# Weights of the S5 scan inside the first feed-forward: products one step later, factors loaded earlier, the steps over 48 weight tiles instead of 32

## The chip, the cores and the metric

The kernel runs on one core of one Trainium2 chip. The metric is device microseconds (us) of one launch; a shorter time is better. Five engines take part: TensorE (PE, matrix products; its weight loads are shown as PEld), VectorE (DVE), ScalarE (ACT), GpSimd (POOL) and SyncE (SP), whose queue issues nearly all transfers. Each engine works through its own list of instructions in a fixed order, and so does each queue of transfers.

## The reference

Two blocks of two layers each act on 256 latent and 256 context tokens of width 1024. The first block ends each layer with a SwiGLU feed-forward, and the second layer of the second block is an S5 state-space mixer. Cut to what matters here:

```python
def _swiglu(h, w_gate, w_up, w_down):
    return (jax.nn.silu(h @ w_gate) * (h @ w_up)) @ w_down

def s5_discretize(a_re, a_im, b_re, b_im, c_re, c_im, log_dt):
...
    a_bar = jnp.exp(dt * a)
    b_bar = ((a_bar - 1) / a)[..., None] * lax.complex(f(b_re), f(b_im))
    c_mat = lax.complex(f(c_re), f(c_im))
    return a_bar, b_bar, c_mat

def s5_scan(u, a_bar, b_bar, c_mat, x0):
...
        bu = jnp.einsum('btgh,gph->btgp', u_blk.astype(jnp.complex64), b_bar)
...
        _, xs = lax.associative_scan(_affine_compose, (a, bu), axis=1)
        y = jnp.einsum('btgp,ghp->btgh', xs, c_mat).real
```

There are two directions, 64 groups of 16 channels and 64 states a group, and the S5 parameters don't depend on the tokens. So the kernel turns the recurrence into blocks of 8 tokens and makes the matrices of these blocks (powers of a_bar times b_bar, c_mat times powers of a_bar, and the products of both) ahead of time, while the first block's first feed-forward runs.

## The kernel before

All products run in float32 split in two parts: `split` (L195, L196) makes `hi` on ScalarE and `lo` on VectorE out of each loaded weight tile, and `mm3` (L205 to L207) multiplies hi by hi, hi by lo and lo by hi. A weight tile is 128 columns of output and up to 8 slices of 128 inputs, so it costs 24 products of 512 tokens each (21 with 7 slices). `linear_steps` runs over the tiles of one weight matrix: it loads and splits a tile, multiplies, hands the sum to a consumer, and then calls `tick`, which runs one step of a generator that lies in the background. The first three tiles of each matrix are multiplied in two halves of 256 tokens.

The first feed-forward (`ffn`, called in `body` with the weights `f0_u`, `f0_d0` to `f0_d2`) has three blocks. Block 0 has 16 gate and up tiles and then 8 down tiles of 8 slices; blocks 1 and 2 have 14 gate and up tiles and 8 down tiles of 7 slices. A gate tile is evicted by ScalarE as `sg` (L1683), an up tile by VectorE (L1687), which ScalarE and VectorE turn into the two parts `hh` (L1694) and `hl` (L1695); the down tiles multiply `hh` and `hl`, and VectorE puts their sums into `y` (L1706, L1708). The feed-forward is called with `ticks=("w", ())`: a tick follows each gate and up tile, and none follows a down tile.

`"w"` is the generator `s5_weights`. It runs over 16 chunks of 4 groups, and in each over two directions `d`. A chunk begins with the load of its factors `bc` (L1443, SP queue, two buffers). One direction is: three VectorE operations that make `Wt` (L1456 twice, L1457); four transposes of `Wt` on TensorE into PSUM (L1460), a copy `wvo` on ScalarE (L1463) and its store `wv` on the SP queue (L1464); three GpSimd operations that make `Ec` (L1471 twice, L1472) and the two stores `wc` of it on the SP queue (L1476); four products of `Ec` with the factors on TensorE (L1479). After the second direction VectorE builds `band` (L1486 to L1489) from these products, and GpSimd issues four stores `tt` of it (L1491). There is one step to each direction, so 32 ticks carry all of it: 16 in block 0, 14 in block 1 and 2 in block 2. The tile names draw on few buffers: two of `Wt` (both are in use while the sum is made), three of `Ec`, two of `bc`, two of `band` and two PSUM banks each of the kinds `pa` (transposes) and `pb` (products).

The order on the engines is not the order of the source: a planner takes the source as a list by priority and puts an instruction on its engine as soon as, by its own estimates, its inputs and buffers are there. That is why the first steps of the generator stand some 60 us ahead of the feed-forward's first tile.

Of the kernel before, what the change touches and what calls it, by code (L numbers as in the profile page):

```python
# [9 lines left out]
F32 = mybir.dt.float32  # L10
# [3 lines left out]
ALU = mybir.AluOpType  # L14
# [3 lines left out]
P = 128  # L18
# [6 lines left out]
SEGS = ((1, 0, CTX), (0, CTX, T))  # L25
# [12 lines left out]
def vw(ap, off, dims):  # L38
    return bass.AP(ap.tensor, ap.offset + off, [ap.ap[0]] + [list(d) for d in dims])
# [89 lines left out]
class Kern:  # L129
# [125 lines left out]
    def load(self, Wd):  # L255
        raw = self.wp.tile(list(Wd.shape), F32, tag="raw", name=self.n("raw"), bufs=4)
        self.nc.sync.dma_start(raw, Wd)
        return raw
# [1043 lines left out]
    def s5_poles(self, pool, sc, par):  # L1302
# [8 lines left out]
        def tt(a, b, op, out=None):  # L1311
            o = t() if out is None else out
            v.tensor_tensor(o, a, b, op)
            return o
# [41 lines left out]

        E = pool.tile([P, 6, 128], F32, tag="E", name="s5E")
        lo, hi = slice(0, 64), slice(64, 128)
        tt(e, co, ALU.mult, E[:, 0])
        ni = tt(e, sn, ALU.mult, sn)  # L1360
# [15 lines left out]
        for i, r, src, sign in ((1, lo, ni, -1.0), (1, hi, ni, 1.0), (2, lo, ph[0], 1.0), (2, hi, ph[1], -1.0),  # L1376
                                (3, lo, ph[1], -1.0), (3, hi, ph[0], -1.0), (4, lo, ph[1], 1.0), (4, hi, ph[0], -1.0),
                                (5, lo, ph[0], 1.0), (5, hi, ph[1], 1.0)):
            nc.scalar.mul(E[r, i], src[r], sign)
        nc.sync.dma_start(sc["E"], E)  # L1380

    def s5_powers(self, pool, sc):
# [4 lines left out]
        def tile(tag, n):  # L1387
            return pool.tile([P, 512], F32, tag=tag, name=self.n("s5p"), bufs=4)[:, :n * 128].rearrange("p (n c) -> p n c", n=n)

        E1, E2, w = tile("Pm", 4), tile("Pm", 2), tile("Pm", 2)  # L1390
        nc.sync.dma_start(E1, sc["E"][:, 0:4])
        nc.sync.dma_start(E2, sc["E"][:, 4:6])

# [41 lines left out]
    def s5_weights(self, pool, sc):  # L1435

        nc, A = self.nc, self.A
        PG = pool.tile([P, 4, 9, 128], F32, tag="PG", name="PGr")
        nc.sync.dma_start(PG, sc["pg"])
        PW, F1, F2 = [PG[:, 0], PG[:, 1]], PG[:, 2], PG[:, 3]  # L1440
        for ch in range(16):
            w = pool.tile([P, 560], F32, tag="bc", name=self.n("bc"), bufs=2)
            nc.sync.dma_start(w, A["s5_w"][ch])  # L1443
            BA = w[:, :160].rearrange("p (d g h) -> p d g h", d=2, g=5)
            BB, CA, CB = (w[:, o:o + 128].rearrange("p (d g h) -> p d g h", d=2, g=4) for o in (160, 288, 416))
            Dd = w[:, 544:560]
            kp = self.psum("pb")
            for d in range(2):
                o = 64 * d + 4 * ch

                base, st = (7 * 128, -128) if d == 0 else (0, 128)
                pw = [vw(PW[i], base + o, [[1, 4], [st, 8], [0, 16]]) for i in range(2)]
                bs = [x[:, d, :4, None, :].to_broadcast([P, 4, 8, 16]) for x in (BA, BB)]
                Wt = [pool.tile([P, 4, 8, 16], F32, tag="Wt", name=self.n("Wt"), bufs=2) for _ in range(2)]
                for i in range(2):
                    nc.vector.tensor_tensor(Wt[i], pw[i], bs[i], ALU.mult)  # L1456
                nc.vector.tensor_tensor(Wt[0], Wt[0], Wt[1], ALU.add)  # L1457
                ps = self.psum("pa")
                for g in range(4):
                    nc.tensor.transpose(ps[:, g * P:(g + 1) * P], Wt[0][:, g].rearrange("p s h -> p (s h)"),  # L1460
                                        self.ident)
                wv = pool.tile([P, 4, 128], F32, tag="wvo", name=self.n("wvo"), bufs=2)
                nc.scalar.copy(wv.rearrange("p g n -> p (g n)"), ps)  # L1463
                nc.sync.dma_start(sc["wv"][ch, :, :, d], wv)  # L1464

                base, st = (0, 128) if d == 0 else (8 * 128, -128)
                ff = [vw(f, base + o, [[1, 4], [st, 9], [0, 16]]) for f in (F1, F2)]
                cs = [x[:, d, :, None, :].to_broadcast([P, 4, 9, 16]) for x in (CA, CB)]
                Ec = [pool.tile([P, 4, 9, 16], F32, tag="Ec", name=self.n("Ec"), bufs=3) for _ in range(2)]
                for i in range(2):  # L1470
                    nc.gpsimd.tensor_tensor(Ec[i], ff[i], cs[i], ALU.mult)  # L1471
                nc.gpsimd.tensor_tensor(Ec[0], Ec[0], Ec[1], ALU.add)  # L1472
                E = Ec[0].rearrange("p g d h -> p g (d h)")
                for r in range(2):
                    rs = slice(64 * r, 64 * r + 64)
                    nc.sync.dma_start(sc["wc"][ch // 2, r, d, :, 4 * (ch % 2):4 * (ch % 2) + 4],  # L1476
                                      E[rs, :, 16:144] if d == 0 else E[rs, :, 0:128])
                for g in range(4):
                    nc.tensor.matmul(kp[32 * g:32 * g + 32, d * P:(d + 1) * P],  # L1479
                                     BA[:, d, g:g + 2, :].rearrange("p g h -> p (g h)"),  # L1480
                                     E[:, g, 0:128] if d == 0 else E[:, g, 16:144], start=True, stop=True,
                                     skip_group_check=True)
                if d == 0:
                    yield
            band = pool.tile([P, 240], F32, tag="band", name=self.n("band"), bufs=2)
            nc.vector.tensor_copy(band[:, 0:128], kp[:, 128:256])  # L1486
            nc.vector.tensor_tensor(band[:, 112:128], band[:, 112:128], Dd, ALU.add)
            nc.vector.tensor_tensor(band[:, 112:128], band[:, 112:128], kp[:, 0:16], ALU.add)
            nc.vector.tensor_copy(band[:, 128:240], kp[:, 16:128])  # L1489
            for j in range(4):  # L1490
                nc.gpsimd.dma_start(sc["tt"][ch // 2, :, :, 4 * (ch % 2) + j].rearrange("s h c -> h s c"),  # L1491
                                    vw(band[32 * j:32 * j + 16], 112, [[-16, 8], [1, 128]]))
            yield

    def s5_shift(self, shift, pool):

# [219 lines left out]
def body(tc, A, out, dbg=None):  # L1716
    with ExitStack() as ctx:
        K = Kern(tc, A, ctx, dbg)
        nc = K.nc
        K.load_pack()  # L1720
        xd = K.dr.tile([P, KT, T], F32, tag="xd", name="xd")
        sc = scratch(K)
        g = K.gains1
# [30 lines left out]
        with tc.tile_pool(name="ffn0", bufs=1) as fp:  # L1754
            x = fp.tile([P, KT, T], F32, tag="x", name="x")
            nc.sync.dma_start(x[:, :, :CTX], A["ctx1"])
            nc.sync.dma_start(x[:, :, CTX:], A["x"])
            y = fp.tile([P, KT, T], F32, tag="y", name="y0")
            acc = K.squares(SEGS)

            def mixed(i, ps, a, b, y=y, acc=acc):
                nc.vector.tensor_copy(y[:, i, a:b], ps)
                K.add_squares(acc, y, i, SEGS, a, b)

            step = K.halves(x, y, acc, lambda: (K.vecP(m0[:, :, 2], g[:, 0, 1]), K.vecA(m0[:, :, 4], g[:, 0, 2], "b"),
                                                m0[:, :, 3]))
            K.linear_fm(A["ew_out"], M, 512, mixed, ends=True, half=lambda: next(step))
            X = next(step)
            y = fp.tile([P, KT, T], F32, tag="y", name="y1")
            part = s1.rearrange("p k c -> p (k c)")[:, :32].rearrange("p (v j) -> p v j", v=2)  # L1770
            K.bg["w"] = K.s5_weights(fp, sc)
            acc = K.squares(SEGS)
            step = K.halves(x, y, acc, lambda: (K.vecP(m0[:, :, 5], g[:, 0, 3]), K.vecA(m1[:, :, 1], g[:, 1, 0], "b"),
                                                m1[:, :, 0]))

            def half():
                K.finish("w")
                next(step)

            K.ffn(X, 512, A["f0_u"], [A[f"f0_d{i}"] for i in range(3)], "swiglu", y, fp, 9,  # L1780
                  lambda k, a, b: K.add_squares(acc, y, k, SEGS, a, b), half=half, ticks=("w", ()))
            X = next(step)
            nc.sync.dma_start(xd[:, :, CTX:], x[:, :, CTX:])
        with tc.tile_pool(name="mix1", bufs=1) as mix:
# [4 lines left out]
        with tc.tile_pool(name="in2", bufs=1) as xp:  # L1789
# [5 lines left out]
            with tc.tile_pool(name="ffn1", bufs=1) as fp:  # L1795
                y = fp.tile([P, KT, LAT], F32, tag="y", name="y0")
                acc = K.squares(LSEG)
# [10 lines left out]
                acc = K.residual_rms(xl, y, K.vecP(m1[:, :, 2], g[:, 1, 1]), LSEG, acc)  # L1808
                X = K.norm_mod(xl, K.vecA(m1[:, :, 4], g[:, 1, 2], "b"), m1[:, :, 3], LSEG, acc)
                grp[1](pool=fp, bufs=8)  # L1810
                y = fp.tile([P, KT, LAT], F32, tag="y", name="y1")
# [11 lines left out]
                acc = K.residual_rms(xl, y, K.vecP(m1[:, :, 5], g[:, 1, 3]), LSEG, acc3)  # L1823
# [292 lines left out]
```

## Time and profile before

| | us |
|---|---|
| median of 3 runs | 2606.03 (2606.03, 2606.04, 2597.53) |
| the profiled execution | 2601.28 |
| its span on the core | 2599.5 |
| TensorE busy | 2427.1 (93%) |
| VectorE busy | 1513.9 (58%) |
| ScalarE busy | 972.1 (37%) |
| GpSimd busy | 514.6 (20%) |

The feed-forward's tiles run from 434 us to 896 us of the span, and the ticks with S5 work from there to 782 us. The profile tells each instruction's start and duration, what its engine waited for ahead of it, and in slices the clock that TensorE was granted (1.00 is full speed). "Busy" counts the time from an instruction's start to its end, including what it waits inside.

### The profile page before, as it was taken

To read this page: it belongs to the slowest core of one execution; us is meant where nothing else is said; L and a number is where in the kernel's file an instruction comes from. 1 tells how busy PE (TensorE), PEld (TensorE's weight loads), DVE (VectorE), ACT (ScalarE), POOL (GpSimd) and SP (SyncE) were. 2 spreads that over 40 slices of the span, in tenths; PEclk is the share of its full clock that TensorE was granted. 3 is DMA by queue.
4 is the path that set the end of the run, shared out by engine and by line. 5 is a ranking of instruction groups with operands and counts; after the bars stand their busy time and mean duration, and the time that the engine had idled before them with its cause. 6 is when DMAs were issued, how large, how long until landed. Compare 5 with 4: busy or idle time off the path is not lost.

```text
span 2599.5 us, 40143 instructions
## 1 busy us (share of the span) xinstructions
PE 2427.1 (93%) x15813; PEld 1979.1 (76%) x15813; DVE 1513.9 (58%) x2897; ACT 972.1 (37%) x1591; POOL 514.6 (20%) x648
## 2 busy tenths in 40 slices
PE   6999989989889998889999999999999999959999
PEld 5875566768678688889699788556888888628999
DVE  5545436865843466674555552665588744485666
ACT  5523323312222253333444453443423224534443
POOL 2910013763710042330100100110100000260000
PEclk9999999989999999999999999999999999989999
DMA  8326673654543332113665522002365533876564
GB/s 284 116 92 223 242 273 100 166 158 122 153 127 100 104 113 98 59 48 105 255 225 181 194 89 82 17 17 74 111 191 178 170 107 96 185 259 220 154 181 152
DMA packets 162925, 378.05 MB, mean 145 GB/s; under 512 B 24144, under 2 KB 70096, under 8 KB 162608
## 3 DMA queue, kind: packets, MB, share of 16 engines
q1 hardware_dynamic: 159728, 368.27, 44.3%
q0 software_dynamic: 3008, 7.21, 1.4%
q8 instruction: 125, 2.05, 0.3%
q14 instruction: 64, 0.52, 0.1%
HBM read 344.75 MB, written 30.67 MB: 144 GB/s over the span
## 4 chain that ended last, share of the span: by engine, by line
PE 73%; DVE 10%; DMA 6%; POOL 5%; ACT 3%; issue 2%; SPq 1%; POOLq 0%; DVEq 0%; ACTq 0%
PE pl L205 17%; PE pl L206 16%; PE pl L207 16%; PE pm L329 3%; POOL Ec L1471 2%; DMA bc<-s_w 2%; DVE lo L196 2%; PE pl L984 2%; PE pa L77 2%; DMA mcol<-ada_t 1%; POOL Ec L1472 1%; PE pl L279 1%; PE pl L280 1%; PE pl L277 1%; DVE pm L395 1%
## 5 line engine op out<-in xcount | busy, mean ns | idle before, releaser
L195 ACT CAST hi<-raw 128x1024 fp32r<-128x1024 f32 (+4 forms) x393 | 400.2, 1020 | 841.9 <-PE pl L206 640.3
L196 DVE TENSOR_TENSOR lo<-raw,hi 128x1024 fp32r<-128x1024 f32 (+4 forms) x393 | 486.6, 1240 | 341.1 <-ACT hi L195 334.9
L206 PE MATMUL pl<-X,hi 128*128 128x256 f32 (+1 forms) x2032 | 654.2, 323 | 5.9 <-POOL X L490 5.7
L205 PE MATMUL pl<-X,hi 128*128 128x256 f32 (+1 forms) x2032 | 657.6, 326 | 1.6 <-ACT X L487 1.6
L207 PE MATMUL pl<-X,lo 128*128 128x256 f32 (+1 forms) x2032 | 652.1, 322 | 1.5 <-DVE lo L196 1.5
L205 PEld LDWEIGHTS pl<-X,hi 128*128 128x128 f32 x2032 | 395.3, 195 | 39.3 <-issue 9.1
L206 PEld LDWEIGHTS pl<-X,hi 128*128 128x128 f32 x2032 | 395.7, 195 | 37.8 <-POOL X L490 8.6
L207 PEld LDWEIGHTS pl<-X,lo 128*128 128x128 f32 x2032 | 396.2, 195 | 33.4 <-issue 4.9
L205 PE MATMUL pl<-hh,hi 128*128 128x256 f32 (+1 forms) x1071 | 330.0, 309 | 10.7 <-ACT hh L1694 10.6
L206 PE MATMUL pl<-hl,hi 128*128 128x256 f32 (+1 forms) x1071 | 328.4, 307 | 8.5 <-DVE hl L1695 8.3
L207 PE MATMUL pl<-hh,lo 128*128 128x256 f32 (+1 forms) x1071 | 326.8, 306 | 0.0
L205 PEld LDWEIGHTS pl<-hh,hi 128*128 128x128 f32 x1071 | 203.7, 191 | 32.2 <-ACT hh L1694 12.2
L206 PEld LDWEIGHTS pl<-hl,hi 128*128 128x128 f32 x1071 | 204.1, 191 | 20.7 <-DVE hl L1695 10.6
L207 PEld LDWEIGHTS pl<-hh,lo 128*128 128x128 f32 x1071 | 204.4, 191 | 10.4 <-DVE y L1708 0.4
L1471 POOL TENSOR_TENSOR Ec<-PGr,bc 128x576 f32<-128x576 f32 x64 | 102.0, 1609 | 181.4 <-DVE lo L196 84.3
L205 PE MATMUL pl<-M,hi 128*128 128x256 f32 (+1 forms) x416 | 125.9, 305 | 6.9 <-ACT hi L195 5.9
L329 PE MATMUL pm<-mraw,s_cc 128*32 128x512 f32 x576 | 116.0, 606 | 10.3 <-DMA mraw<-ada_w 9.8
L207 PE MATMUL pl<-M,lo 128*128 128x256 f32 (+1 forms) x416 | 123.1, 297 | 1.2 <-DVE lo L196 1.2
L206 PE MATMUL pl<-M,hi 128*128 128x256 f32 (+1 forms) x416 | 123.5, 298 | 0.2 <-DVE M L856 0.2
L1708 DVE TENSOR_TENSOR y<-y,pl 128x256 f32<-128x256 f32 (+1 forms) x86 | 45.2, 526 | 127.2 <-PE pl L207 126.9
L490 POOL TENSOR_TENSOR X<-nt,X 128x256 fp32r<-128x256 f32 x48 | 37.4, 781 | 379.7 <-ACT nt L489 379.7
L395 DVE SCALAR_TENSOR_TENSOR pm<-mcol,mrow 128x512 f32<-128x512 f32 x128 | 89.3, 698 | 36.1 <-DMA mcol<-ada_t 22.4
(515 smaller groups left out, 3757.7 us busy)
## 6 DMA issues: line engine op xcount, KB each, us to landing
mraw<-mod_w SPq DMA_DIRECT2D x96, 512.0 KB, 5.5
raw<-f_u SPq DMA_DIRECT2D x88, 512.0 KB, 3.8
mraw<-ada_w SPq DMA_DIRECT2D x64, 512.0 KB, 6.3
raw<-p_u SPq DMA_DIRECT2D x64, 512.0 KB, 3.6
raw<-p_d SPq DMA_DIRECT2D x64, 512.0 KB, 3.6
raw<-ow_fm SPq DMA_DIRECT2D x32, 512.0 KB, 3.3
mcol<-ada_t SPq DMA_DIRECT2D x64, 256.0 KB, 3.1
raw<-f_d SPq DMA_DIRECT2D x32, 448.0 KB, 3.3
```

Source lines behind the costliest of these rows:

```text
L77: K.nc.tensor.matmul(self.ps[32 * j:32 * j + 32, :N], K.ones[:rows, :32], self.sq[:rows, :N], start=k < 4, stop=k + 4 >= self.kt, skip_gro ...
L195: nc.scalar.copy(hi, raw)
L196: nc.vector.tensor_tensor(lo, raw, f32(hi), ALU.subtract)
L205: mm(out, w[0][:, kw, wsl], xh, start=first and a == 0, stop=False, skip_group_check=True)
L206: mm(out, w[0][:, kw, wsl], xl, start=False, stop=False, skip_group_check=True)
L207: mm(out, w[1][:, kw, wsl], xh, start=False, stop=last and a == nk - 1, skip_group_check=True)
L329: nc.tensor.matmul(ps[32 * j:32 * j + 32, :], s[:, k, :], raw[:, jj * 512:(jj + 1) * 512], start=k == 0, stop=k == KT - 1, skip_group_chec ...
L395: nc.vector.scalar_tensor_tensor(self.psum("pm"), buf[:, n % 2], 1.0, s[:, v], ALU.mult, ALU.mult, accum_out=(dst if h else part)[:, v, j: ...
L490: nc.gpsimd.tensor_tensor(lo[:, k, a:b], t, f32(hi[:, k, a:b]), ALU.subtract)
L984: nc.tensor.matmul(ps[:, :nk], q[:, tt * P:(tt + 1) * P], k[:, :nk], start=True, stop=True)
L1471: nc.gpsimd.tensor_tensor(Ec[i], ff[i], cs[i], ALU.mult)
L1708: nc.vector.tensor_tensor(y[:, c, a0:b0], y[:, c, a0:b0], ps, ALU.add)
```

## The change

`s5_weights` is cut in two. A new function `products` holds the transposes, the copy and store of `wvo`, the stores `wc`, the products of `Ec`, and after the second direction `band` and the stores `tt`. A step now first runs `products` for the step before it, and then makes `Wt` and `Ec` of its own; the last products follow the loop. The load of `bc` is taken out of the chunk's head: the first stands ahead of the loop, and each next chunk's is issued in the second direction's step of the chunk before it, behind the products of that step. After a second direction there are two yields instead of one, so that a chunk takes three ticks (two with work, one empty), and the feed-forward is called with ticks after down tiles too: 48 ticks and a last one, over 16 + 8 + 14 + 8 tiles and the first three of block 2.

```diff
-        for ch in range(16):
+        def load(ch):
             w = pool.tile([P, 560], F32, tag="bc", name=self.n("bc"), bufs=2)
             nc.sync.dma_start(w, A["s5_w"][ch])
...
+            return w
+
+        def products(ch, Wt, E, BA, Dd, kps):
+            if not kps:
+                kps.append(self.psum("pb"))
+            kp, d = kps[0], len(kps) - 1
+            kps.append(None)
+            ps = self.psum("pa")
+            for g in range(4):
+                nc.tensor.transpose(ps[:, g * P:(g + 1) * P], Wt[:, g].rearrange("p s h -> p (s h)"), self.ident)
+            wv = pool.tile([P, 4, 128], F32, tag="wvo", name=self.n("wvo"), bufs=2)
+            nc.scalar.copy(wv.rearrange("p g n -> p (g n)"), ps)
+            nc.sync.dma_start(sc["wv"][ch, :, :, d], wv)
+            for r in range(2):
+                rs = slice(64 * r, 64 * r + 64)
+                nc.sync.dma_start(sc["wc"][ch // 2, r, d, :, 4 * (ch % 2):4 * (ch % 2) + 4],
+                                  E[rs, :, 16:144] if d == 0 else E[rs, :, 0:128])
+            for g in range(4):
+                nc.tensor.matmul(kp[32 * g:32 * g + 32, d * P:(d + 1) * P],
...
+            if d == 0:
+                return
             band = pool.tile([P, 240], F32, tag="band", name=self.n("band"), bufs=2)
...
-            yield
+
+        w, last = load(0), None
+        for ch in range(16):
...
+            kps = []
+            for d in range(2):
+                if last is not None:
+                    products(*last)
+                if d and ch < 15:
+                    w = load(ch + 1)
...
+                last = ch, Wt[0], Ec[0].rearrange("p g d h -> p g (d h)"), BA, Dd, kps
+                yield
+                if d:
+                    yield
+        products(*last)
...
-                  lambda k, a, b: K.add_squares(acc, y, k, SEGS, a, b), half=half, ticks=("w", ()))
+                  lambda k, a, b: K.add_squares(acc, y, k, SEGS, a, b), half=half, ticks=("w", "w"))
```

No operation is added or removed; the buffers and their numbers stay as they were.

## Rows read from the trace of the kernel before

**Rows 1.** The page's chain that ended last, shares by engine.
```profile
PE 73%; DVE 10%; DMA 6%; POOL 5%; ACT 3%; issue 2%; SPq 1%; POOLq 0%; DVEq 0%; ACTq 0%
```
**Rows 2.** Stretches: busy us (x count) of PE, PEld, DVE, ACT, POOL; granted clock; DMA.
```profile
461.00:513.00 52.00, 51.60 (x287) 40.31 (x280) 45.59 (x53) 17.25 (x26) 38.20 (x32) 1.00 0.66 187
513.00:575.00 62.00, 48.73 (x245) 37.96 (x244) 45.17 (x49) 12.84 (x19) 45.59 (x37) 0.83 0.52 138
...
671.00:732.00 61.00, 47.73 (x250) 37.32 (x250) 45.72 (x50) 13.65 (x19) 46.28 (x38) 0.86 0.51 134
```
**Rows 3.** Timeline of TensorE: start, us, line, out<-in, [idle before <-releaser].
```profile
461.09 0.50 PE L205 MATMUL pl<-X,hi 128*128 128x512 f32 x1
...
500.56 0.50 PE L205 MATMUL pl<-X,hi 128*128 128x512 f32 x1
...
506.15 0.60 PE L1460 MATMUL pa<-pack_sb,Wt 128*128 128x128 f32 x4
...
507.03 0.50 PE L205 MATMUL pl<-X,hi 128*128 128x512 f32 x1
...
549.40 0.63 PE L1460 MATMUL pa<-pack_sb,Wt 128*128 128x128 f32 x4 [2.23 <-DVE Wt L1457]
...
560.26 0.39 PE L205 MATMUL pl<-hh,hi 128*128 128x256 f32 x1
...
569.28 0.58 PE L206 MATMUL pl<-hl,hi 128*128 128x256 f32 x1 [3.84 <-DVE hl L1695]
...
619.87 0.38 PE L205 MATMUL pl<-X,hi 128*128 128x256 f32 x1
...
715.45 0.39 PE L205 MATMUL pl<-hh,hi 128*128 128x256 f32 x1
```
**Rows 4.** Timeline of VectorE: evictions of the first two down tiles, blocks 0 and 1.
```profile
574.67 0.69 DVE L1706 COPY y<-pl 128x512 f32<-128x512 f32 x1 [2.10 <-PE pl L207]
...
580.00 0.69 DVE L1706 COPY y<-pl 128x512 f32<-128x512 f32 x1 [3.13 <-PE pl L207]
...
731.04 0.69 DVE L1708 TENSOR_TENSOR y<-y,pl 128x512 f32<-128x512 f32 x1 [2.00 <-PE pl L207]
...
735.47 0.69 DVE L1708 TENSOR_TENSOR y<-y,pl 128x512 f32<-128x512 f32 x1 [2.56 <-PE pl L207]
```
**Rows 5.** Timeline of GpSimd over one chunk, up to the next chunk's first operation.
```profile
508.58 3.38 POOL L1471 TENSOR_TENSOR Ec<-PGr,bc 128x576 f32<-128x576 f32 x2 [4.62 <-DMA bc<-s_w]
...
517.23 2.29 POOL L1472 TENSOR_TENSOR Ec<-Ec,Ec 128x576 f32<-128x576 f32 x1
519.45 2.11 POOL L1491 DMA_DIRECT2D tt<-band  x4
527.18 3.37 POOL L1471 TENSOR_TENSOR Ec<-PGr,bc 128x576 f32<-128x576 f32 x2 [5.62 <-DMA bc<-s_w]
```
**Rows 6.** Timeline of the SP queue at the end of that chunk.
```profile
519.54 1.26 SPq L1476 DMA_DIRECT2D wc<-Ec  x2
520.90 0.71 SPq L1443 DMA_DIRECT2D bc<-s_w  x1
```
**Rows 7.** Instructions by tile name: durations in ns, minimum/median/maximum.
```profile
L1471 POOL TENSOR_TENSOR Ec<-PGr,bc x64: 1221/1669/1890, 369.5 to 726.7; 128x576 f32<-128x576 f32 x64
L1472 POOL TENSOR_TENSOR Ec<-Ec,Ec x32: 1421/1758/2297, 374.4 to 728.6; 128x576 f32<-128x576 f32 x32
...
L1456 DVE TENSOR_TENSOR Wt<-PGr,bc x64: 677/693/1921, 369.4 to 770.9; 128x512 f32<-128x512 f32 x64
```
**Rows 8.** Groups by shape in block 2 (790 to 844 us): busy, mean ns.
```profile
L196 DVE TENSOR_TENSOR lo<-raw,hi 128x1024 fp32r<-128x1024 f32 x8 | 9.8, 1226 | 15.0 <-ACT hi L195 14.4
...
L1695 DVE TENSOR_TENSOR hl<-sg,hh 128x512 fp32r<-128x512 f32 x5 | 3.4, 684 | 0.0
```
**Rows 9.** Chain of waits, 441 to 452 us: first and last of four.
```profile
442.27 1.62 POOL Ec L1471
...
449.99 1.48 POOL Ec L1472
```

More of the change, by code (lines that the diff above doesn't have):

```diff
@@ L1440, in s5_weights @@
         PW, F1, F2 = [PG[:, 0], PG[:, 1]], PG[:, 2], PG[:, 3]
-        for ch in range(16):
+        def load(ch):
             w = pool.tile([P, 560], F32, tag="bc", name=self.n("bc"), bufs=2)
             nc.sync.dma_start(w, A["s5_w"][ch])
+            return w
[16 more added lines that the diff above has]
+                nc.tensor.matmul(kp[32 * g:32 * g + 32, d * P:(d + 1) * P],
+                                 BA[:, d, g:g + 2, :].rearrange("p g h -> p (g h)"),
+                                 E[:, g, 0:128] if d == 0 else E[:, g, 16:144], start=True, stop=True,
+                                 skip_group_check=True)
+            if d == 0:
+                return
+            band = pool.tile([P, 240], F32, tag="band", name=self.n("band"), bufs=2)
+            nc.vector.tensor_copy(band[:, 0:128], kp[:, 128:256])
+            nc.vector.tensor_tensor(band[:, 112:128], band[:, 112:128], Dd, ALU.add)
+            nc.vector.tensor_tensor(band[:, 112:128], band[:, 112:128], kp[:, 0:16], ALU.add)
+            nc.vector.tensor_copy(band[:, 128:240], kp[:, 16:128])
+            for j in range(4):
+                nc.gpsimd.dma_start(sc["tt"][ch // 2, :, :, 4 * (ch % 2) + j].rearrange("s h c -> h s c"),
+                                    vw(band[32 * j:32 * j + 16], 112, [[-16, 8], [1, 128]]))
+        w, last = load(0), None
+        for ch in range(16):
             BA = w[:, :160].rearrange("p (d g h) -> p d g h", d=2, g=5)
@@ L1446, in s5_weights @@
             Dd = w[:, 544:560]
-            kp = self.psum("pb")
+            kps = []
             for d in range(2):
+                if last is not None:
+                    products(*last)
+                if d and ch < 15:
+                    w = load(ch + 1)
                 o = 64 * d + 4 * ch
@@ L1457, in s5_weights @@
                 nc.vector.tensor_tensor(Wt[0], Wt[0], Wt[1], ALU.add)
[L1458 to L1464, printed above, removed]
                 base, st = (0, 128) if d == 0 else (8 * 128, -128)
@@ L1472, in s5_weights @@
                 nc.gpsimd.tensor_tensor(Ec[0], Ec[0], Ec[1], ALU.add)
[L1473 to L1483, printed above, removed]
-                    yield
[L1485 to L1492, printed above, removed]
-            yield
+                last = ch, Wt[0], Ec[0].rearrange("p g d h -> p g (d h)"), BA, Dd, kps
+                yield
+                if d:
+                    yield
+        products(*last)
     def s5_shift(self, shift, pool):
```

## The prediction

> **What bounds the kernel now.** I read the chain of waits on the page first. TensorE holds 73% of it, and all other engines and transfers share the rest [rows 1]; so a change off TensorE pays only where TensorE waits for it. The second view is busy time by stretch in the feed-forward that the change touches. Early in block 0 TensorE is busy 51.60 of 52.00 us at a granted clock of 1.00, the upper of its two levels (2.4 GHz). In the rest of block 0 it is busy 48.73 of 62.00 at a mean of 0.83, and late in block 1 47.73 of 61.00 at 0.86, so part of it at the lower level (1.2 GHz); GpSimd is busy some 46 us of each [rows 2]. The reader is to see that the same tiles with the same ticks run without a gap at first and with gaps later: something falls behind tick by tick.
>
> The third view, TensorE's timeline, prices it. A tile with its tick takes 507.03 - 500.56 = 6.47 us, of which the tick's products take 507.03 - 506.15 = 0.88. Later the transposes wait 2.23 us for `Wt` (549.40), and at the block's end a product waits 3.84 us for `hl` (569.28) [rows 3].
>
> GpSimd and the SP queue tell why. One chunk's two `Ec` run from 508.58 to 519.52, 10.9 us. Only then do the two `wc` stores go (519.54), the `bc` load stands behind them in the queue (520.90), and GpSimd starts the next chunk at 527.18, 6.3 us after the load's issue, having waited 5.62 for it [rows 5, 6]. This is a closed ring: load, `Ec`, `wc`, load. It turns in 527.18 - 508.58 = 18.6 us, and the two tiles that it has to keep up with take 12.9. The planner's early steps give it a lead; once that is used up, TensorE and VectorE run at the ring's pace.
>
> **What is lost now.** From the rows, against tiles at 6.47:
> - Block 0, tiles 4 to 16: 560.26 - 461.09 = 99.2 us for 13 tiles, against 84.1: 15.1 lost [rows 3].
> - Its first down tile: 560.26 to the eviction at 574.67 is 14.4, against 5.3 between the next two: 9.1 lost [rows 3, 4].
> - Block 1, tiles 2 to 14: 715.45 - 619.87 = 95.6 against 84.1: 11.5 lost [rows 3].
> - Its first down tile: 731.04 - 715.45 = 15.6 against 4.4: 11.2 lost [rows 3, 4].
>
> Together 46.9 us, TensorE's low clock in these stretches included. Block 2 has two ticks with work and no such loss.
>
> **The change, part by part.** *Steps over three ticks a chunk.* GpSimd's work for a chunk, 10.9 us of `Ec` and 2.1 us of issuing `tt` [rows 5], makes 13.0; the time for it becomes three tiles, of which two have products: 3 x 5.59 + 2 x 0.88 = 18.5 us (5.59 is 6.47 - 0.88), and about 3 x 4.4 + 1.8 = 15.1 in block 1's down tiles [rows 3, 4]. Even the unbroken ring of 18.6 nearly fits the former. TensorE's own products are the same number, so what moves into the down tiles costs there what it gives back here: nothing in sum.
>
> *The load ahead.* It leaves the ring: it is issued behind the products of the first direction, one chunk early, some two tiles (12 us) before it is wanted, against 6.3 us to arrive [rows 5, 6]. Its buffer is that of the chunk before, whose last reader is the `band` sum, one tick earlier. What it is moved past on the SP queue are the two `wc` stores of the second direction and one `wv` store. If the cover went, GpSimd would wait as it does now, 5.62 us a chunk.
>
> *Products a step behind.* The transposes and the `Ec` products then find inputs made a tile (6.47 us) earlier, so the waits of 2.23 and the like go. What is late next? VectorE's second `Wt` product needs the buffer that the transposes of the step before free, and these now stand behind the current tile: VectorE can wait there, and the `hl` and `lo` behind it. A `lo` is made up to two tiles ahead (three buffers), so it has the time; an `hl` is wanted at once only where a block ends. The `wc` stores also go a step later, so an `Ec` buffer is held one tick longer; three suffice, as one step's sum and the next step's pair are three.
>
> *Block ends.* `hl` of the last up tile is read late in the first down tile, some 4.9 of its 5.3 us in, and both last tiles (ticks 16 and 38) carry work. From nothing to the 3.84 that is waited there now [rows 3]; I take half, 2 us at each of two ends, 4 in all, as VectorE's queue is shorter but not empty.
>
> *The start.* Four `Ec` operations of the early steps lie on the chain ahead of the norm's last parts, 5.8 us (1.62 to 1.48 each) [rows 9]. Where the planner puts them after the change no row tells: they may leave the chain (5.8 gained) or as many more may come (5.8 lost). I take nothing, since the steps' inputs and GpSimd's free time there don't change.
>
> *Sum.* 46.9 - 4 = 42.9 us off the profiled execution: 2601.28 - 42.9 = 2558.4 (its span is 2599.5 of that). The three runs have a mean of 2603.2, 1.9 above the profiled one, and a median 4.7 above; with 1.9 I forecast 2560.
>
> **VectorE against GpSimd.** Rows first: `Ec` products take 1.22 us at best and 1.67 at the median, `Wt` products 0.68 at best and up to 1.92 [rows 7], while a `lo` takes 1.23 in block 2, where GpSimd is idle [rows 8]. So the two engines stretch each other. The Trainium skill (SBUF — State Buffer, section "Who interferes with whom") says that a VectorE operation with two SBUF inputs and a GpSimd operation that reads SBUF take turns at one port pair, as under a lock. It speaks against moving work under the down tiles, where VectorE was alone; the rows just named agree with it as far as they go.
>
> **Rivals.**
> 1. *The pair becomes the bound.* If VectorE and GpSimd operations can't overlap at all, their shortest times add up: before 7.7 (GpSimd, a chunk) + 2 x 1.23 + 6 x 0.68 + 0.68 = 14.9 in 12.9 us; after 7.7 + 3 x 1.23 + 6 x 0.68 + 1.5 x 0.68 = 16.5 in 18.5 [rows 7, 8]. That fits, with 2.0 to spare. With GpSimd's 10.9 us as seen [rows 5] it is 19.7: 1.2 us over in each of 10 chunks under gate and up tiles, and some 2 in the 2.7 chunks of block 1's down tiles, 17 in all: 2577. For it: the stretching; against it: 45.59 and 38.20 us of busy time lie in 52 us without a gap on TensorE [rows 2], so they do overlap. 12%.
> 2. *Block ends stay as they are.* VectorE puts the step's `Wt` ahead of `hl`, and 20.3 us remain: 2601.3 - 26.6 + 1.9 = 2577. For it: that is the order at 569.28; against it: the queue there was late already. 10%.
> 3. *Slower.* GpSimd takes the `tt` stores of the last chunk in source order, ahead of the next `Ec`. Then products 0.88, `band` (1 to 6 us in VectorE's queue), `tt` 2.1 and `Ec` 5.5 (half of 10.9) make 9.5 to 14.5 us, and the products of the first direction want it one tile, 6.47 us, later: TensorE waits 3 to 8 us in each of 16 chunks, 48 to 128, in the middle 88. 2601.3 - 42.9 + 88 = 2646; it decides as soon as that wait passes 2.7 us a chunk. Against it: the `tt` at 519.45 follows at once on the `Ec` that ended at 519.52, whose products and `band` still had to come, so it belongs to the chunk before and stands behind both `Ec` of the next one [rows 5]; the planner doesn't wait for it. 6%.
> 4. *It doesn't do what it says:* the planner pulls the load or the products back to where they were. Then the ring of 18.6 stays, against 18.5 a chunk, and block 1's down tiles lose 3.5 us in 2.7 chunks, 9: 2569, still faster. 6%.
>
> **How the numbers follow.** My forecast of 2560 has 66%. Its own bounds: all 46.9 and the 5.8 of the start gained, at the lowest run's offset (-3.8): 2546; 5.8 lost and the block ends whole (3.7 more), at the median's offset: 2573. Rivals 1 and 2 at the median's offset reach 2580, and a little of each together 2583. So 2546 to 2583, which leaves out rival 3 and what is unknown. About 0.5% (13 us) is what a measurement here can tell from no change. Faster 91%, same 3%, slower 6%.
>
> **What would show it.** Right: in the stretches of [rows 2] TensorE is busy without gaps at clock 1.00, GpSimd's operations no longer name `bc` as releaser, `bc` is issued ahead of the second direction's `Ec`, and the transposes wait for nothing. Rival 1 shows as GpSimd or VectorE near full and tiles above 6.47; rival 2 as `hl` waits at the two ends; rival 3 as `Ec` waits under `pb` products. Wrong would be a loss far from this feed-forward, from a planner that orders other stages anew; no row here can exclude it.

## The result and the profile after

The changed kernel takes 2571.6 us (median of four runs, 2566.3 to 2572.5) beside 2601.8 for the kernel before: a ratio of 0.987, interval 0.9845 to 0.9894. Measured again beside three variants it is 2564.7 against 2606.9, a ratio of 0.9841, interval 0.982 to 0.9863. So it is faster by 1.3 to 1.6%, 30 to 42 us. The forecast of 2560 took 42.9 us off the profiled execution of before; both results lie in the range given, 12 and 5 us above the forecast.

The page's chain by engine, to be laid beside [rows 1]. TensorE's share rose from 73 to 79%, GpSimd's fell from 5 to 1%.

```profile
PE 79%; DVE 10%; DMA 4%; ACT 3%; issue 2%; POOL 1%; SPq 0%; DVEq 0%; ACTq 0%; POOLq 0%
```

The same stretches as in [rows 2], with the same columns (PE, PEld, DVE, ACT and POOL busy, granted clock, DMA share, GB/s):

```profile
461.00:513.00 52.00, 52.00 (x274) 41.29 (x273) 40.31 (x43) 15.13 (x22) 32.82 (x29) 1.00 0.60 176
513.00:575.00 62.00, 60.60 (x383) 51.08 (x382) 49.77 (x51) 15.74 (x21) 36.76 (x32) 1.00 0.58 165
671.00:732.00 61.00, 57.71 (x386) 49.34 (x385) 47.94 (x57) 13.72 (x19) 39.73 (x35) 0.97 0.59 165
```

TensorE, busy 48.73 of 62 at 0.83 before, is busy 60.60 at 1.00. GpSimd is busy less, not more. The view of waits from 450 to 760 us (who waits <- for whom: us in total, times, longest) held these rows before:

```profile
POOL Ec L1471 <- DMA bc<-s_w: 51.0, 13, 5.6
...
PE pa L1460 <- DVE Wt L1457: 11.4, 10, 2.2
...
PE pl L206 <- DVE hl L1695: 6.8, 2, 3.8
...
PE pb L1479 <- POOL Ec L1472: 3.0, 6, 0.6
```

After the change it holds one cause for TensorE:

```profile
PE pl L206 <- DVE hl L1713: 4.7, 2, 3.3
...
POOL Ec L1505 <- PE pb L1464: 77.2, 15, 11.7
POOL tt L1476 <- DVE band L1474: 39.6, 16, 14.2
POOL Ec L1505 <- DMA bc<-s_w: 4.2, 4, 2.1
```

TensorE's waits for `Wt` and for `Ec` are gone. GpSimd waits for `bc` 4.2 us where it waited 51.0, and idles instead for the buffers that the lagged products free (`pb`) and for `band`, at no cost, as the timeline of one chunk shows (GpSimd, VectorE, SP queue and TensorE, in order of time):

```profile
513.38 1.23 POOL L1505 TENSOR_TENSOR Ec<-PGr,bc 128x576 f32<-128x576 f32 x1
...
518.83 0.69 DVE L1497 TENSOR_TENSOR Wt<-PGr,bc 128x512 f32<-128x512 f32 x1 [2.54 <-PE pa L1455]
519.26 1.35 POOL L1505 TENSOR_TENSOR Ec<-PGr,bc 128x576 f32<-128x576 f32 x1 [4.65 <-PE pb L1464]
...
520.69 1.75 POOL L1506 TENSOR_TENSOR Ec<-Ec,Ec 128x576 f32<-128x576 f32 x1
521.08 1.39 DVE L1472 TENSOR_TENSOR band<-band,bc 128x16 f32<-128x16 f32 x1
...
522.54 0.33 SPq L1444 DMA_DIRECT2D bc<-s_w  x1
522.97 1.43 SPq L1461 DMA_DIRECT2D wc<-Ec  x2
...
524.17 2.11 POOL L1476 DMA_DIRECT2D tt<-band  x4 [1.73 <-DVE band L1474]
...
525.19 0.32 PE L1464 MATMUL pb<-Ec,bc 128*32 128x128 f32 x4
...
526.30 1.25 POOL L1505 TENSOR_TENSOR Ec<-PGr,bc 128x576 f32<-128x576 f32 x1
```

The `bc` load now leaves ahead of the `wc` stores (522.54 against 522.97), as soon as `band` has read the old factors. The sum of the first direction ends at 522.44, the product that reads it starts at 525.19: GpSimd's wait of 4.65 us ahead of that sum leaves 2.75 to spare. The `tt` issue of the chunk before (524.17) stands between this chunk's two directions.

**Where the time went, by the feed-forward's marks.** Seven starts cut it into parts: the second sigmoid, the eighth, block 0's first eviction, block 1's first sigmoid, its seventh, its first eviction, and the last one (timeline of ScalarE and VectorE, kernel after):

```profile
459.07 0.59 ACT L1701 ACTIVATE sg<-pl 128x512 f32<-128x512 f32 x1
...
532.10 0.59 ACT L1701 ACTIVATE sg<-pl 128x512 f32<-128x512 f32 x1
...
544.89 0.69 DVE L1724 COPY y<-pl 128x512 f32<-128x512 f32 x1 [1.23 <-PE pl L207]
...
595.31 0.59 ACT L1701 ACTIVATE sg<-pl 128x512 f32<-128x512 f32 x1
...
669.21 0.59 ACT L1701 ACTIVATE sg<-pl 128x512 f32<-128x512 f32 x1
...
685.99 0.69 DVE L1726 TENSOR_TENSOR y<-y,pl 128x512 f32<-128x512 f32 x1 [2.14 <-PE pl L207]
...
855.68 0.42 DVE L1726 TENSOR_TENSOR y<-y,pl 128x256 f32<-128x256 f32 x1 [0.74 <-PE pl L207]
```

Twelve tiles lie between the second and eighth sigmoid, and again in block 1 between the first and seventh; at 6.47 us each, a tick in all of them and no wait, they take 77.6. The same marks in the one profile of every kernel, in us (a ratio is to the kernel before, with its interval):

| kernel | 12 tiles, block 0 | to first eviction | down tiles, block 0 | 12 tiles, block 1 | to first eviction | second sigmoid to last eviction | ratio of times |
|---|---|---|---|---|---|---|---|
| before | 86.9 | 26.6 | 45.4 | 84.7 | 26.3 | 434.3 | 1 |
| after | 73.0 | 12.8 | 50.4 | 73.9 | 16.8 | 396.6 | 0.987 [0.9845, 0.9894] |
| after, again (e5) | 73.0 | 12.9 | 50.4 | 73.9 | 19.3 | 399.5 | 0.9841 [0.982, 0.9863] |
| spread alone (e1) | 75.2 | 13.3 | 50.4 | 75.7 | 13.6 | 397.0 | 0.9857 [0.9829, 0.9886] |
| load alone (e2) | 79.8 | 23.4 | 45.4 | 79.2 | 25.3 | 417.5 | 0.9936 [0.9917, 0.9955] |
| load and lag (e3) | 81.1 | 17.3 | 45.5 | 87.7 | 16.7 | 413.9 | 0.9912 [0.9875, 0.9949] |
| lag alone (e4) | 81.1 | 17.2 | 45.5 | 81.7 | 15.4 | 406.2 | 0.992 [0.9892, 0.9948] |
| spread and load (e6) | 75.2 | 13.3 | 50.4 | 75.7 | 13.7 | 397.4 | 0.9862 [0.9838, 0.9885] |
| spread and lag (e7) | 73.0 | 12.9 | 50.4 | 73.9 | 16.9 | 396.8 | 0.9845 [0.9821, 0.9869] |
| after, empty steps moved (e8) | 72.6 | 12.4 | 51.4 | 73.9 | 15.1 | 397.0 | 0.9822 [0.98, 0.9845] |
| after, moved otherwise (e9) | 72.6 | 12.4 | 51.4 | 72.9 | 11.3 | 392.5 | 0.9807 [0.9783, 0.9831] |
| e3 with less for VectorE (e10) | 84.4 | 27.1 | 45.5 | 87.1 | 23.2 | 433.4 | 0.9975 [0.9956, 0.9994] |
| ticks in down tiles only (e11) | 86.3 | 26.5 | 64.7 | 95.9 | 10.3 | 446.1 | 1.0024 [1.0004, 1.0044] |
| spread alone, moved as e9 (e12) | 73.9 | 12.8 | 51.2 | 74.4 | 11.3 | 395.3 | 0.9833 [0.9808, 0.9858] |

Two profiles of the same kernel (after and e5) agree within 0.3 us in every part but one: block 1's end, 16.8 and 19.3.

### The profile page after: what moved, and what is told of

Read it like the earlier page. It is cut to its first block, busy times and chain, and to the rows that moved or that the text cites. A ratio compares the mean times of both kernels' runs of the same rounds, so it can differ in the third digit from the quotient of the medians.

```text
span 2563.7 us, 40161 instructions
## 1 busy us (share of the span) xinstructions
PE 2414.7 (94%) x15813; PEld 1970.4 (77%) x15813; DVE 1518.1 (59%) x2897; ACT 971.3 (38%) x1591; POOL 503.0 (20%) x648
## 4 chain that ended last, share of the span: by engine, by line
PE 79%; DVE 10%; DMA 4%; ACT 3%; issue 2%; POOL 1%; SPq 0%; DVEq 0%; ACTq 0%; POOLq 0%
PE pl L205 18%; PE pl L206 18%; PE pl L207 17%; PE pm L329 3%; PE pl L984 2%; PE pa L77 2%; DVE lo L196 2%; DMA mcol<-ada_t 2%; PE pl L279 1%; PE pl L280 1%; DVE pm L395 1%; PE pl L277 1%; PE pb L77 1%; PE pa L661 1%; PE pl L1006 1%
## 5 line engine op out<-in xcount | busy, mean ns | idle before, releaser
L196 DVE TENSOR_TENSOR lo<-raw,hi 128x1024 fp32r<-128x1024 f32 (+4 forms) x393 | 496.6, 1265 | 332.2 <-ACT hi L195 330.2
L207 PEld LDWEIGHTS pl<-X,lo 128*128 128x128 f32 x2032 | 392.5, 193 | 31.5 <-issue 4.9
L1505 POOL TENSOR_TENSOR Ec<-PGr,bc 128x576 f32<-128x576 f32 x64 | 95.5, 1503 | 169.8 <-DMA bc<-s_w 89.0
L329 PE MATMUL pm<-mraw,s_cc 128*32 128x512 f32 x576 | 115.7, 606 | 11.3 <-DMA mraw<-ada_w 10.9
L490 POOL TENSOR_TENSOR X<-nt,X 128x256 fp32r<-128x256 f32 x48 | 37.5, 781 | 382.7 <-ACT nt L489 382.7
```

The costliest lines, as they stand in the source:

```text
L196: nc.vector.tensor_tensor(lo, raw, f32(hi), ALU.subtract)
L207: mm(out, w[1][:, kw, wsl], xh, start=False, stop=last and a == nk - 1, skip_group_check=True)
L329: nc.tensor.matmul(ps[32 * j:32 * j + 32, :], s[:, k, :], raw[:, jj * 512:(jj + 1) * 512], start=k == 0, stop=k == KT - 1, skip_group_chec ...
L490: nc.gpsimd.tensor_tensor(lo[:, k, a:b], t, f32(hi[:, k, a:b]), ALU.subtract)
```

## Experiments

The first four are told by the feed-forward's time from its first product, the others from the second sigmoid. The second measure is the better one: the first product drifts (427.0 to 435.3 us among these kernels), and ahead of the second sigmoid TensorE still waits for parts of the norm (`X`, L490).

**e1, the spread alone.** To the kernel before, behind the last yield of a chunk and in the call (cut):

```diff
+            yield
-  half=half, ticks=("w", ()))
+  half=half, ticks=("w", "w"))
```

> The kernel before with the spread alone: a third, empty step behind each chunk and ticks in the down tiles too (48 ticks); load at the chunk's head, products beside their own step's factors. Compared by the first feed-forward's own time, from its first product to its last y eviction: 461.2 us before, 422.7 after. Theory: the ring (load, Ec, wc stores, next load) turns in 18.6 us a chunk and now has three tiles, 18.5 to 19.4 us, so it all but fits: TensorE's waits for Ec in the tiles between go, the stretch is 423 to 435 us and the whole some 2570 us. Rival: the order of the queue and of the engines is what costs, and a chunk still waits whatever its length: products still stand behind their own factors, each of 32 working ticks makes TensorE wait, the stretch stays at 442 us or more (2585 us or more).

Measured: 424.0 us by that measure, and 2567.0 us, as the theory said. The ring is whole in this kernel and all but fits three tiles: the view of waits shows GpSimd waiting 13.9 us for `bc` in place of 51.0, and TensorE little.

```profile
PE pl L206 <- DVE hl L1696: 3.7, 2, 1.9
PE pa L1460 <- DVE Wt L1457: 2.8, 4, 0.7
...
POOL Ec L1471 <- DMA bc<-s_w: 13.9, 12, 3.1
```

Of the three parts of the change this one alone brings 37.3 of the 37.7 us gained between second sigmoid and last eviction (34.8 by the changed kernel's other profile, e5).

**e2, the load alone.** `w = load(0)` ahead of the loop, and in it, ahead of a direction's work:

```diff
+                if d and ch < 15:
+                    w = load(ch + 1)
```

> The kernel before with the load alone moved: a chunk's factors are loaded between the two directions of the chunk ahead; still 32 ticks, two tiles a chunk, products beside their own factors. Theory of the ring alone: with the store no longer ahead of the load GpSimd needs 13.0 us a chunk and two tiles are 12.9, so the tiles between lose next to nothing (26.6 us back) and the two block ends stay (20 us): stretch about 435 us, whole about 2575. Rival, the pair: GpSimd's and VectorE's shared work is 14.9 us in a chunk of 12.9, so two thirds or more of the tiles' loss stays and the stretch is 450 to 461 us (2590 to 2602). Rival, the transposes' and products' waits for their own step's Wt and Ec count for themselves: 445 us or more.

Measured: 444.8, between the expectations; the parts tell them apart. The 24 tiles lose 3.8 us against 77.6 each dozen, where before lost 16.4; so what they lost was mostly the ring, and the pair's rival, by which two thirds stay, falls. The block ends take 48.6 us, 52.9 before, and TensorE still waits 8.3 us for `Wt` and 1.1 for `Ec` (11.4 and 3.0 before): the third rival fits what is left. The edit did less than its theory asked for. GpSimd still waits for `bc`, 34.5 us, because the load stands between the two `wc` stores of the second direction on the SP queue (509.81, load 510.49, 511.11): the ring is not open but shorter, 532.08 - 515.42 = 16.7 us from one chunk's first `Ec` to the next one's, where it was 18.6.

**e3, load and lag without the spread.** To the changed kernel:

```diff
                 yield
-                if d:
-                    yield
-  half=half, ticks=("w", "w"))
+  half=half, ticks=("w", ()))
```

> The changed kernel without the spread: load ahead and products a step behind, 32 ticks in gate and up tiles alone. If length of a chunk is what counts, GpSimd (13.0 us plus its waits for the buffers and for the band) doesn't fit into two tiles of 12.9 and the stretch is 440 to 461 us, whole 2580 to 2602. If order and lag are what counts, the stretch is within 6 us of the changed kernel's 422.7, less the products that the down tiles don't carry: 420 to 429 us, whole 2565 to 2575.

Measured: 439.4 and 2583.9 us (single runs from 2566.5 to 2608.5), next to the first expectation's range. The tiles lose 3.5 us in block 0 and 10.1 in block 1. GpSimd hardly waits for `bc` (1.3 us), so the ring is open. But its chunks still lie 501.82 - 487.81 = 14.0 us apart, against 12.9 for two tiles: its operations stand back to back but for 1.73 us ahead of `tt`, where it waits for `band` from VectorE. And VectorE is full as well. The stretch from 500 to 551 us in this kernel:

```profile
500.00:551.00 51.00, 46.23 (x265) 37.09 (x264) 49.39 (x50) 13.71 (x20) 44.18 (x38) 0.97 0.69 198
```

and how VectorE comes to be full, in the timeline of VectorE and GpSimd ahead of a wait of 2.21 us of TensorE for `Wt`:

```profile
602.93 3.48 DVE L1497 TENSOR_TENSOR Wt<-PGr,bc 128x512 f32<-128x512 f32 x1
603.44 2.42 POOL L1505 TENSOR_TENSOR Ec<-PGr,bc 128x576 f32<-128x576 f32 x2
605.94 1.77 POOL L1506 TENSOR_TENSOR Ec<-Ec,Ec 128x576 f32<-128x576 f32 x1
606.34 2.45 DVE L196 TENSOR_TENSOR lo<-raw,hi 128x1024 fp32r<-128x1024 f32 x1
```

A `Wt` product of 0.68 us at best takes 3.48 beside two `Ec` products in a row. That is rival 1's mechanism, at two tiles a chunk: VectorE stands beside GpSimd's `Ec`, and GpSimd's `tt` waits for VectorE's `band`.

**e4, the lag alone.** As e3, and `w = load(ch)` at the chunk's head instead of one ahead.

> The kernel before with the lag alone: TensorE's products of a step are issued a step later, the load stays at the chunk's head, 32 ticks. Theory: the ring is still closed (load, Ec, wc stores, which now come a step later, next load behind them in SP's queue), and turns no faster: stretch 456 to 470 us, whole 2596 to 2612; the later stores may even lengthen it. Rival: TensorE's own waits are the loss, and a lag takes them away: stretch 440 to 448 us, whole 2580 to 2588.

Measured: 431.8, below both, so the expectation misread the queue. With the lag the stores of a second direction are issued a step later, behind the next chunk's load; the lag opens the ring by itself. The view of waits has 1.1 us of GpSimd for `bc`, and VectorE is as full as it can be:

```profile
500.00:551.00 51.00, 48.37 (x278) 37.50 (x279) 50.90 (x53) 15.57 (x23) 43.17 (x36) 1.00 0.64 182
```

So the lag opens the ring, the load alone shortens it, and the spread makes the chunk as long as the ring. The first two leave a bound behind them; the spread also makes room for the pair: VectorE is busy 39.56 of the same 51 us with the spread alone, and 43.78 in the changed kernel.

**e5 to e7, the changed kernel again, without the lag, and without the load ahead.** e6 is e1 and e2 together; e7 is the changed kernel with `w = load(ch)` at the chunk's head.

> The changed kernel once more, beside the next three on one chip. From the second sigmoid of the first feed-forward to its last y eviction it took 396.6 us (434.3 before, 397.0 with the spread alone). Expected again: 394 to 400 us, whole 0.985 to 0.989 of the kernel before.

> The changed kernel without the lag: spread and load ahead, each step's products beside their own factors. If the spread does all and the lag nothing: within 3 us of the changed kernel (396.6 us in the stretch, 0.987 of before). If the lag guards TensorE from waits for Wt and Ec, the waits of the spread alone (2.8 us for Wt in four places) come back, and more at the block ends: 400 to 406 us, some 0.989.

> The changed kernel without the load ahead: spread and lag, load at the chunk's head. Theory: a lag already takes the load out from behind the second direction's stores, so the load ahead adds nothing here: stretch within 2 us of the changed kernel's 396.6. Rival: the load at the head of the chunk makes GpSimd wait for its landing in each of 16 chunks (13.9 us of such waits with the spread alone) and that reaches TensorE: 400 to 410 us.

Measured: 399.5, 397.4 and 396.8 us in the stretch; the three ratios' intervals overlap. Leaving the load ahead out changes no part by more than 0.1 us against the first profile of the changed kernel: beside spread and lag it does nothing that can be measured. Leaving the lag out costs 4.0 us in the 24 tiles (75.2 + 75.7 against 73.0 + 73.9), where four waits of 0.7 us for `Wt` return, and gives back 3.1 at block 1's end; in the whole stretch it costs nothing that can be measured here.

**e8 and e9, empty steps behind the last up tiles.** To the changed kernel, in `s5_weights` (cut); in e9 the list is `[*range(1, 35, 3), 36, 38, 41, 45]`:

```diff
-        w, last = load(0), None
+        w, last, n = load(0), None, 0
+        empty = [*range(1, 35, 3), 38, 41, 44, 47]
...
+                n += 1
+                while n in empty:
+                    yield
+                    n += 1
                 if last is not None:
...
                 yield
-                if d:
-                    yield
```

> The changed kernel with its empty steps moved so that ticks 16 and 38, the ones behind the last gate and up tile of each block, are empty (48 steps, 32 of them at work, as before). Theory: the wait for hl at each block end (1.4 and 3.3 us, and half clock behind the second, together 8 us over a loss-free end) comes from lo and hl on VectorE standing beside this tick's own Wt and Ec; with the tick empty 5 to 8 us of it go: stretch 389 to 392 us, whole 5 to 8 us under the changed kernel. Rival: VectorE is late at the block end from the ticks ahead of it, or the planner brings other steps' work there: stretch 395 to 400 us, no difference.

> The changed kernel with the empty steps placed so that ticks 16 and 38 are empty and no three working steps stand in a row while gate and up tiles run (empty: 1, 4, ... 34, 36, 38, 41, 45; three in a row at 42 to 44, in down tiles). With ticks 35 to 37 all at work TensorE waited 2.0 us for Wt and ran the next 24 products in 7.33 us instead of 5.74. Theory (VectorE beside GpSimd is what is late): this wait and the half clock go, stretch from the second sigmoid to the last y eviction 392 to 395 us (397.0 before that), whole 3 us under the first arrangement. Rival: the three working steps in the down tiles cost the same there: 396 to 399 us.

In e8 the `hl` waits shrink from 4.7 us to 0.6, but steps 35, 36 and 37 all work, and there a `Wt` comes late (TensorE's timeline, and the stretch behind it):

```profile
663.97 0.63 PE L1455 MATMUL pa<-pack_sb,Wt 128*128 128x128 f32 x4 [2.00 <-DVE Wt L1503]
```

```profile
664.00:668.00 4.00, 4.00 (x20) 2.95 (x21) 3.92 (x5) 0.58 (x1) 2.86 (x2) 0.62 0.32 92
```

The expected 5 to 8 us did not come: 397.0, in the rival's range. The two ends give back 2.1 us, but the down tiles, which now carry more of the working steps, take 3.0 more (51.4 for 50.4, and 171.7 for 169.7 from block 1's first eviction to the last one). e9 spaces these steps and puts the three in a row under down tiles. All that TensorE then waits for from 450 to 760 us:

```profile
PE pl L206 <- DVE hl L1716: 0.6, 1, 0.6
PE pa L1455 <- DVE Wt L1503: 0.2, 1, 0.2
```

The stretch is 392.5 us, as expected, and the time 2556.1 (2552.1 to 2559.1), the lowest of all. Its ratio's interval lies below that of the first measurement of the changed kernel and overlaps that of the second (e5) by 0.0011, so the few us between the two rest on the trace and not on the times.

**e10, load and lag with less work for VectorE.**

```diff
-                for i in range(2):
-                    nc.vector.tensor_tensor(Wt[i], pw[i], bs[i], ALU.mult)
-                nc.vector.tensor_tensor(Wt[0], Wt[0], Wt[1], ALU.add)
+                nc.vector.tensor_tensor(Wt[0], pw[0], bs[0], ALU.mult)
```

> The kernel with load ahead and lag and no spread, with two of VectorE's three instructions for Wt left out (the second product and the sum: the wv rows are then not those of the reference); GpSimd's work is whole. With them the six pairs of tiles between the second and the eighth sigmoid took 81.1 us, those of the second block 87.7, against 77.6 for tiles with a tick and no loss. Theory, the pair: VectorE and GpSimd together have 14.9 us to do in a chunk of 12.9; less VectorE work, no loss: 77 to 79 us in both. Rival, GpSimd alone (13.0 us in 12.9 and its waits): loss stays, 80 to 88 us.

Measured: 84.4 and 87.1 us, no gain, and a ratio of 0.9975 (e3: 0.9912). This does not settle the pair, for the edit did more than it should: the planner set the load behind a `wc` store again (SP queue), and GpSimd waits for `bc` 32.2 us (view of waits), with e3 at 1.3:

```profile
507.11 0.58 SPq L1461 DMA_DIRECT2D wc<-Ec  x1
507.79 0.57 SPq L1444 DMA_DIRECT2D bc<-s_w  x1
```

```profile
POOL Ec L1503 <- DMA bc<-s_w: 32.2, 12, 4.2
```

It shows the ring once more: with VectorE's stretch down to 31.66 us busy of 51 the loss of the kernel before is back. How much of e3's and e4's loss is VectorE's and how much GpSimd's stays open.

**e11, ticks in the down tiles without a third step.** The second line of e1's edit alone.

> The kernel before with the ticks in the down tiles too, but no third step: a chunk still has two tiles, 32 ticks are used up in the second block's gate and up tiles. Theory, the length of a chunk: block 0's tiles lose as before (86.9 us for six pairs, 26.6 us at its end), and the four chunks in the down tiles, each needing 18.6 us in 11, lose some 5 to 7 us each, while half of block 1's tiles and its end have no work and lose nothing (20 us back): whole 2590 to 2610. Rival, it is room in the down tiles that the spread uses: the down tiles lose nothing, whole 2575 to 2585.

Measured: 2612.1 us, no gain, and 2 us above the theory's range. Block 0 loses as before, and its down tiles take 64.7 us instead of 45.4. GpSimd's timeline there shows two chunks one ring apart, 593.73 - 574.53 = 19.2 us:

```profile
574.53 3.38 POOL L1471 TENSOR_TENSOR Ec<-PGr,bc 128x576 f32<-128x576 f32 x2 [4.17 <-DMA bc<-s_w]
...
593.73 3.37 POOL L1471 TENSOR_TENSOR Ec<-PGr,bc 128x576 f32<-128x576 f32 x2 [6.20 <-DMA bc<-s_w]
```

So the gain of the spread is the length of a chunk, not room under the down tiles by itself. The theory had half of block 1's tiles free of loss; its 12 tiles take 95.9 us instead of 84.7 all the same, since those with work go at the ring's pace, 17.6 to 19.0 us for two. Block 1's end without a working tick takes 10.3 us here, another measure of a free end.

**e12, the spread alone with e9's empty steps.**

> The kernel before with spread alone, empty steps placed as in the changed kernel's second arrangement (no lag, no load ahead). If lag and load ahead add nothing, it is within 2 us of the changed kernel so arranged (392 to 396 us in the stretch). If they matter once the block ends are clear, by the four waits for Wt (0.7 us each, 2.8 together) and the ring at 18.6 us in two working steps that follow each other: 396 to 402 us.

Measured: 395.3 us, inside the first range and 2.8 above e9, where 2 was expected at most, and five waits for `Wt` of 3.6 us together where e9 has 0.2:

```profile
PE pa L1465 <- DVE Wt L1462: 3.6, 5, 0.9
```

So the lag, with the load ahead, is worth about 3 us once the block ends are clear; that rests on the waits, for the times (0.9833 against 0.9807) can't tell the two apart.

## Why the prediction was right, and where its sizes were off

**The account.** From the first-eviction marks and TensorE's first tiles, by the prediction's own parts, the profiled executions differ up to the last eviction by 39.8 us (895.5 against 855.7), where 42.9 was forecast:
- *Tiles between, 26.6 lost:* all back. Block 0's tiles 4 to 16 went from 99.2 us to 79.4, block 1's 2 to 14 from 95.6 to 80.6; that is 34.8, and the 8.2 beyond the loss are products that moved to the down tiles (eight or nine steps at 0.88 us).
- *"Nothing in sum" for the moved products:* about right. The other tiles pay 10.3 for those 8.2, so 2.1 are lost.
- *Block ends, 20.3 lost and 4 to stay:* mis-sized. By the prediction's yardstick 2.1 of 9.1 stay in block 0 and 5.9 of 11.2 in block 1, 8.0 together.
- *The start, taken at 0:* tile 4 begins 3.05 us earlier (458.04 against 461.09). A part of this has a cause: two of the four `Ec` operations of [rows 9] have left the chain of waits, and the two that stay take 2.6 us in place of 5.8 (1.23 at 444.59, 1.37 at 446.50). It is the same in e5 and e7, while in e1, without the lag, all four are there. How large the part is stays open: in e5 the second sigmoid comes 5.7 us earlier still than in the other profile of the same kernel.

26.6 - 2.1 + (20.3 - 8.0) + 3.05 = 39.85. The profiles as wholes differ by only 35.0 us (2601.28 and 2566.27), because the part behind the last eviction took 2599.5 - 895.5 = 1704.0 us in the profile of before and 1708.0 after. The instructions there stand in the same order on every engine in both kernels, but for two products of TensorE that stand a few places apart. Over all fourteen profiles this part runs from 1704.0 to 1713.2, and that of before is the lowest, so I take it for variation and not for the change. The same holds for medians, where two measurements of the same pair of kernels give 30 and 42 us. The prediction's offset of 1.9 us stood for this variation and was too small for it. The lower end of its range is a slip of sum: 2601.28 - 46.9 - 5.8 - 3.8 is 2545, not 2546.

**Why the block ends kept twice what was forecast.** Block 1's end in the changed kernel, timeline of VectorE, GpSimd and TensorE in order of time, and, second, the stretches behind it:

```profile
672.56 1.08 DVE L196 TENSOR_TENSOR lo<-raw,hi 128x896 fp32r<-128x896 f32 x1
...
675.71 0.38 PE L205 MATMUL pl<-hh,hi 128*128 128x256 f32 x1
676.30 3.39 DVE L196 TENSOR_TENSOR lo<-raw,hi 128x896 fp32r<-128x896 f32 x1
676.32 2.41 POOL L1505 TENSOR_TENSOR Ec<-PGr,bc 128x576 f32<-128x576 f32 x2
678.81 2.14 POOL L1506 TENSOR_TENSOR Ec<-Ec,Ec 128x576 f32<-128x576 f32 x1
679.62 1.88 DVE L1713 TENSOR_TENSOR hl<-sg,hh 128x512 fp32r<-128x512 f32 x1
681.55 0.58 PE L206 MATMUL pl<-hl,hi 128*128 128x256 f32 x1 [3.29 <-DVE hl L1713]
```

```profile
682.00:685.00 3.00, 3.00 (x17) 3.00 (x17) 1.81 (x2) 0.00 (x0) 0.57 (x1) 0.53 0.42 116
685.00:688.00 3.00, 3.00 (x29) 3.00 (x28) 1.78 (x2) 0.95 (x1) 0.00 (x0) 1.00 0.00 0
```

A `lo` of this shape takes 1.08 us alone and 3.39 beside two `Ec` products; `hl` takes 1.88 for 0.68. The two are 3.5 us longer than alone, and TensorE stands 3.29 us. Behind that it runs 3 us near the lower level of its clock (0.53) with 17 matmuls in place of 29, which costs another 1.2. The prediction priced the wait, and left out both VectorE's stretched operations there and what the clock adds. It also read the cover wrong: it has this `hl` read 4.9 us into the first down tile. That tile runs in two halves of 256 tokens, and the first half already reads it: TensorE stood there at 681.55 - 3.29 = 678.26, 2.6 us after the tile's first product. It had the rule for the stretching: the Trainium skill (SBUF — State Buffer, section "Who interferes with whom") has such a pair of operations exclude each other for a whole instruction. The rows agree, and go on: here the VectorE operation lasts past both `Ec` products, not one. In e9, whose tick at that place is empty, the `lo` and the `hl` there take 1.09 and 0.68 us (664.22, 665.23), and the end takes 11.3 us instead of 16.8.

**The other steps.**
- *The ring* was right in kind: shortened by the load alone, it gives back 12.6 of 16.4 us in the tiles (e2), and where it is closed the loss is there (e10, e11). But the prediction hung its opening on the load ahead. The load alone doesn't open it (e2) and does nothing beside the other two parts (e7); the lag opens it (e4), which the prediction did not see, though it wrote that the `wc` stores go a step later.
- *Three tiles a chunk* was put as room for 13.0 us of GpSimd, with the remark that even the unbroken ring nearly fits. e1 shows that remark to be the main thing.
- *The cover of the load,* taken as 12 us, is 8.6 (issued at 522.54 once `band` has read its buffer; next wanted at 531.18). It suffices.
- *Three `Ec` buffers suffice:* only in the result. GpSimd does wait for them, 77.2 us in 15 waits, with 2.75 us to spare in the chunk shown.
- *The lag* was to remove the waits for `Wt`; it does, but they are 2.8 us once a chunk has three tiles (e1).

**The rivals.** The pair (1) did not bind: a tile with its tick still takes 6.47 us (transposes at 499.82 and 506.29), VectorE is busy 43.78 of 51. With two tiles it is full (e3, e4), so the prediction named the right danger, and its sum of 16.5 in 18.5 rightly placed the changed kernel on the safe side. The block ends (2) stayed in part, 8.0 of 20.3. The slower case (3) did not come. The argument against it had `tt` behind both `Ec` of the next chunk; it stands behind the first direction's only, ahead of the second's. That does no harm, for the second's is not wanted for another 11 us (526.30 against products at 537.10). The planner pulled neither load nor products back (4); and the 9 us that this rival gave block 1's down tiles for an unbroken ring didn't show in e1, whose way from block 1's first eviction to the last one is 168.8 us, against 169.7 after the change.

## What to carry to other kernels

When background work falls behind tick by tick, write down its cycle with all queue entries in it and compare that with the ticks it is given; one more tick a cycle can do what a reordering does, and it also makes room for the bound that comes next. Try the parts of such a change one at a time: here the smallest edit carried the gain. Then look at the places where the foreground has no slack, such as the last operand of a block, and leave the tick there empty.

## What the runs showed of the hardware

- A VectorE operation with two inputs, issued beside two GpSimd operations back to back, waits out both: 3.39 us for 1.08 (block 1's end after the change), 3.48 for 0.68 (e3), 3.53 for a `lo` of 1.08 in e8.
- TensorE resumed at a lower granted clock behind gaps of 3.29 us (0.53 over the next 3 us) and 2.00 us (0.62 over the next 4), and at 1.00 behind one of 1.73 (e1, block 1's end). In the first of these the lower clock cost about 1.2 us (17 matmuls in place of 29 in 3 us) beside the wait's 3.29.
- The part of this program behind the feed-forward took 1704.0 and 1708.0 us in two kernels with all but the same order of instructions there, 1708.0 and 1710.0 in two profiles of one kernel, and up to 1713.2 among fourteen.
